# The second layer's down projection by seven block products instead of eight

## The chip, the cores and the metric

One core of a Trainium2 chip. The time is the device time of one execution in microseconds. TensorE (PE) multiplies matrices, VectorE (DVE), ScalarE (ACT) and GpSimd (POOL) work on rows of 128 partitions, and SyncE (SP) issues most of the transfers (DMAs). Each engine runs its own list of instructions in order and waits on semaphores for the others.

## The reference

Two layers of a backbone over 512 tokens of 1024 channels, batch 1. Each layer is a mixer (layer 0: long convolution and neighbourhood attention; layer 1: Conformer convolution) and then a feed-forward part, each between two RMS norms with shift, scale and gate. The change is in the feed-forward part of layer 1:

```python
def conv_ffn(t, w_up, w_dw, b_dw, w_down):
    z = dwconv(t @ w_up, w_dw, b_dw)          # (512, 1024) @ (1024, 5632), 3 taps over tokens
    g, u = jnp.split(z, 2, axis=-1)
    return (jax.nn.silu(g) * u) @ w_down      # (512, 2816) @ (2816, 1024)
...
        y = conv_ffn(hn, ffn_w_up[layer], ffn_w_dw[layer], ffn_b_dw[layer], ffn_w_down[layer])
        h = h + gate2 * rms_norm(y, g_ffn_post[layer])
    return h
```

All is float32.

## The kernel before

**Products.** A float32 operand is cast to the type `float32r` (`hi`), and what the cast leaves off is kept as a second `float32r` tile (`lo`). `mm3` makes one product of three matmuls, hi x hi, hi x lo and lo x hi, lines 284 to 286, accumulated in PSUM. A matmul has 128 rows of the contraction, 128 columns of one operand and 512 of the other.

**The stream of weights.** `Stream` holds all weight tiles of the kernel in the order of their use, each 128 x 1024 (512 KB). `load` (line 295) has SP read a tile into one of 3 buffers `raw`; `split` casts it on ScalarE (line 301, `hi`) and subtracts on VectorE (line 305, `lo`) into two of the 8 buffers `w`, so that four weight tiles are held. `get(n)` hands out the next tile and splits n tiles ahead, with three loads ahead of that. Tiles that have to stay (`wkeep`, named `wk`) go to other pools.

**The feed-forward part, `ffn(l, ...)`.** The up part makes 22 channel blocks i, each with a gate tile and a value tile: 24 matmuls into `pz`, then the 3-tap convolution (ScalarE line 983, VectorE 984 and 985), Silu (1383) and the product into `gu` (1387), where `gu[j]` holds blocks 2j and 2j+1 as 128 channels x 512 tokens. The down part is `gemm_td`: `act(k)` splits one block of `gu` into `gs` (lines 1420, 1421). For the first 16 blocks k, each weight tile serves all four chunks of 128 tokens and both halves of 512 outputs, 24 matmuls; for the last 6 (`KEEP`), the tiles are kept and the chunks are finished one after the other, in two halves of 18 matmuls each. `acc` are the eight PSUM tiles. When chunk t is done, `after(t, acc[t])` calls `post_chunk`: the square sum on ScalarE (line 426), the root on GpSimd (417, 421), the gain and the sum with `h` on VectorE (555, 560), and the output is sent (621).

**Order.** `bg` is a list of generators, of which `bg_step(n)` runs n steps: a weight tile of the up part is followed by two steps (`nbg` = 2). In layer 1 the list holds `mod_gate(1, 2)`, which reads 8 tiles of 512 KB by way of `raw`. A scheduler puts the instructions of each engine into an order from a timeline of its own; inside `tc.manual_schedule` an engine keeps the order of the code.

Of the kernel before, what the change touches and what calls it, by code (L numbers as in the profile page):

```python
# [239 lines left out]
def backbone_kernel(ctx: ExitStack, tc: tile.TileContext, a, cols, out, dump=None, stop=None, mark=lambda s: None):  # L240
# [51 lines left out]

    def load(src):
        r = rpool.tile([P, 1024], F32, name=nm("raw"), tag="raw")
        SP.dma_start(r, src)
        return r

    def split(r, alloc):
        mk = alloc or (lambda: w4(F32R, (P, 1024)))
# [1 line left out]
        A.copy(hi, r)  # L301
        with ExitStack() as queued:
            if behind:
                queued.enter_context(tc.issue_after(behind[0]))
            V.tensor_tensor(lo, r, f(hi), op=ALU.subtract)  # L305
# [165 lines left out]
    def mod_gate(l, which):  # L471
        p0 = 2 if which == 1 else 5
        binit = s4(F32, (P, 1024), "binit")
        G.memset(binit, 0.0)
# [898 lines left out]
        return  # L1373


    def ffn(l, hT, late, after, nxt, nbg):
# [37 lines left out]
        dmp(f"gu{l}", gu[0])  # L1414
        mark(f"down{l}")

        def act(k):
# [2 lines left out]
            A.copy(t_[:, 0], src)  # L1420
            V.tensor_tensor(t_[:, 1], src, f(t_[:, 0]), op=ALU.subtract)  # L1421
# [241 lines left out]
```

## Time and profile before

| | us |
|---|---|
| median of 3 runs | 1251.58 (1250.80 to 1252.73) |
| profiled execution | 1254.67 |
| its span, first to last instruction | 1252.9 |
| busy in the span: PE / DVE / ACT / POOL | 1238.9 / 815.9 / 509.2 / 81.2 |
| mean granted TensorE clock | 0.999 |
| first matmul of the layer 1 down part, from the span's start | 1126.37 |

Rows of the profile are in microseconds from the span's start. "L284 PE MATMUL acc<-w,gs" is an instruction of line 284 on TensorE that writes the tile `acc` from `w` and `gs`; "<-" in brackets names what ended the wait ahead of it. A busy time counts overlapping work of one engine once.

### The profile page before, as it was taken

How to read it: one execution, taken by the hardware profiler on the slowest of the kernel's cores; microseconds unless marked ns; L12 is line 12 of the kernel's file. 1: busy time of each engine (PE TensorE's matmuls, PEld its weight loads, DVE VectorE, ACT ScalarE, POOL GpSimd, SP SyncE). 2: the span in 40 equal slices, each digit the busy share in tenths (PEclk: the TensorE clock that was granted, in tenths of full speed). 3: DMA queues.
4: the chain of work that ended last, by engine and by line, in shares of the span. 5: the costliest groups of instructions: out<-in, count | busy, mean ns of one | idle time of the engine just before them, and what ended most of it. 6: DMA issues, size and time to landing. Idle time of an engine off the chain costs nothing.

```text
span 1252.9 us, 15592 instructions
## 1 busy us (share of the span) xinstructions
PE 1238.9 (99%) x6090; PEld 1028.7 (82%) x6090; DVE 815.9 (65%) x1085; ACT 509.2 (41%) x794; POOL 81.2 (6%) x151
## 2 busy tenths in 40 slices
PE   9999999999999999999999999999999999999997
PEld 6688888888898888787888888887988888888886
DVE  6577795876567788778534567787687555565223
ACT  6543234575353332436223442234534333344221
POOL 3300000241200000000000100001100000000001
PEclk9999999999999999999999999999999999999999
DMA  9546334734036577764334332120264333333221
GB/s 349 199 137 183 120 116 158 234 139 141 29 113 210 182 239 233 235 202 149 118 115 154 103 126 68 34 87 32 83 224 147 101 97 91 99 101 101 86 83 67
DMA packets 48089, 171.82 MB, mean 137 GB/s; under 512 B 5771, under 2 KB 5899, under 8 KB 48016
## 3 DMA queue, kind: packets, MB, share of 16 engines
q1 hardware_dynamic: 47652, 170.10, 42.1%
q8 instruction: 48, 0.79, 0.2%
q0 software_dynamic: 176, 0.40, 0.1%
q10 hardware_dynamic: 188, 0.33, 0.1%
q14 instruction: 25, 0.20, 0.0%
HBM read 167.92 MB, written 2.10 MB: 136 GB/s over the span
## 4 chain that ended last, share of the span: by engine, by line
PE 70%; DMA 12%; DVE 11%; ACT 3%; issue 3%; POOL 0%; SPq 0%; DVEq 0%; POOLq 0%; ACTq 0%
PE pz L284 10%; PE pz L285 10%; PE pz L286 10%; PE acc L286 8%; PE acc L285 8%; PE acc L284 8%; DMA raw<-in_wup 4%; DVE w L305 4%; DMA raw<-in_wcol 3%; DMA raw<-in_wgate 3%; PE pg L284 2%; PE pg L286 2%; PE pg L285 2%; ACT w L301 2%; DVE acc L448 2%
## 5 line engine op out<-in xcount | busy, mean ns | idle before, releaser
L286 PE MATMUL pz<-hTh,w 128*128 128x512 f32 (+1 forms) x920 | 345.3, 376 | 0.9 <-DVE w L305 0.9
L285 PE MATMUL pz<-hTl,w 128*128 128x512 f32 (+1 forms) x920 | 345.4, 376 | 0.0
L284 PE MATMUL pz<-hTh,w 128*128 128x512 f32 (+1 forms) x920 | 344.8, 377 | 0.6 <-DVE hTh L539 0.5
L305 DVE TENSOR_TENSOR w<-raw,w 128x1024 fp32r<-128x1024 f32 x159 | 193.9, 1222 | 200.3 <-ACT w L301 199.9
L301 ACT CAST w<-raw 128x1024 fp32r<-128x1024 f32 x159 | 166.5, 1051 | 337.8 <-PE pz L285 130.6
L286 PEld LDWEIGHTS pz<-hTh,w 128*128 128x128 f32 x920 | 173.8, 189 | 33.1 <-DVE w L305 1.8
L284 PEld LDWEIGHTS pz<-hTh,w 128*128 128x128 f32 x920 | 173.0, 189 | 31.3 <-DVE hTh L539 1.0
L285 PEld LDWEIGHTS pz<-hTl,w 128*128 128x128 f32 x920 | 173.8, 189 | 30.2 <-DVE hTl L540 0.4
L448 DVE SCALAR_TENSOR_TENSOR acc<-raw,sc,acc 128x1024 f32<-128x1024 f32 x74 | 95.0, 1284 | 44.5 <-DMA raw<-in_wcol 24.8
L285 PE MATMUL acc<-w,gs 128*128 128x512 f32 x256 | 99.6, 389 | 0.0
L286 PE MATMUL acc<-w,gs 128*128 128x512 f32 x256 | 98.4, 390 | 0.4 <-DVE gs L1421 0.4
L284 PE MATMUL acc<-w,gs 128*128 128x512 f32 x256 | 97.0, 389 | 0.0
L983 ACT ACTIVATE cv<-pz,pk 128x512 f32<-128x512 f32 x88 | 67.5, 773 | 0.0
L985 DVE SCALAR_TENSOR_TENSOR cv<-pz,pk,cv 128x511 f32<-128x511 f32 x88 | 65.5, 747 | 1.8
L984 DVE SCALAR_TENSOR_TENSOR cv<-pz,pk,cv 128x511 f32<-128x511 f32 x88 | 65.1, 744 | 0.2 <-ACT cv L983 0.2
L1383 ACT ACTIVATE cv<-cv 128x512 f32<-128x512 f32 x44 | 27.7, 629 | 81.3 <-DVE cv L985 81.2
L305 DVE TENSOR_TENSOR wk<-raw,wk 128x1024 fp32r<-128x1024 f32 x30 | 36.4, 1221 | 32.4 <-ACT wk L301 32.2
L286 PEld LDWEIGHTS acc<-w,gs 128*128 128x128 f32 x256 | 48.0, 188 | 10.7 <-DVE gs L1421 0.8
L284 PEld LDWEIGHTS acc<-w,gs 128*128 128x128 f32 x256 | 48.1, 188 | 10.2 <-DVE cv L985 0.2
L285 PEld LDWEIGHTS acc<-w,gs 128*128 128x128 f32 x256 | 48.0, 188 | 9.9
L555 DVE TENSOR_TENSOR py<-acc,gg 128x512 f32<-128x512 f32 x32 | 21.9, 687 | 46.9 <-ACT py L426 46.9
L301 ACT CAST wk<-raw 128x1024 fp32r<-128x1024 f32 x30 | 31.3, 1050 | 46.7 <-DMA raw<-in_wdn 27.3
(329 smaller groups left out, 1909.4 us busy)
## 6 DMA issues: line engine op xcount, KB each, us to landing
raw<-in_wup SPq DMA_DIRECT2D x88, 512.0 KB, 3.6
raw<-in_wcol SPq DMA_DIRECT2D x48, 512.0 KB, 4.2
raw<-in_wdn SPq DMA_DIRECT2D x44, 512.0 KB, 3.6
raw<-in_wgate SPq DMA_DIRECT2D x32, 512.0 KB, 4.3
raw<-in_pw SPq DMA_DIRECT2D x24, 512.0 KB, 4.3
raw<-in_win SPq DMA_DIRECT2D x20, 512.0 KB, 3.8
land<-in_wmod SPq DMA_DIRECT2D x16, 512.0 KB, 10.9
BM<-in_rpb SPq DMA_DIRECT2D x8, 512.0 KB, 4.2
```

The costliest lines, as they stand in the source:

```text
L284: PE.matmul(o, ah, bh, start=start, stop=False)
L285: PE.matmul(o, ah, bl, start=False, stop=False)
L286: PE.matmul(o, al, bh, start=False, stop=stop)
L301: A.copy(hi, r)
L305: V.tensor_tensor(lo, r, f(hi), op=ALU.subtract)
L448: V.scalar_tensor_tensor(acc, rs[k], ck_, init if k == 0 else acc, op0=ALU.mult, op1=ALU.add)
L555: V.tensor_tensor(p_[:, sl], y2[i], gg[:, sl], op=ALU.mult)
L983: A.activation(dst, pz, AF.Identity, bias=pc(bk, i), scale=pc(wk + "1", i))
L984: V.scalar_tensor_tensor(dst[:, 1:w], pz[:, 0:w - 1], pc(wk + "0", i), dst[:, 1:w], op0=ALU.mult, op1=ALU.add)
L985: V.scalar_tensor_tensor(dst[:, 0:w - 1], pz[:, 1:w], pc(wk + "2", i), dst[:, 0:w - 1], op0=ALU.mult, op1=ALU.add)
L1383: A.activation(cv[:, 0], cv[:, 0], AF.Silu, bias=0.0, scale=1.0)
```

## The change

Only the down part of layer 1 is changed. The 512 x 2816 activation A and the 2816 x 1024 weight B are cut into 2 x 2 blocks: tokens 0 to 255 and 256 to 511 (`H0`, `H1`), even and odd channel blocks (`gu[j][:, 0]`, `gu[j][:, 1]`), outputs 0 to 511 and 512 to 1023. Winograd's form of Strassen's scheme gives the four blocks of the result by seven products of 256 x 1408 by 1408 x 512 instead of eight, from sums of blocks. Three of the products take blocks of B as they are, four take sums (`PRODUCTS`).

- **Weights.** `wdb` holds the blocks in device memory, 128 x 5632 each. `sums_down()` makes the four sums in device memory, in six pieces of 1024 columns (the last 512): SP copies a block, and GpSimd issues a DMA that adds another block to it. It is a second generator in `bg`, 10 steps for a piece, 60 in all. A weight tile is now 128 x 1024 of one block, two k-blocks side by side, and each product has six, of which the last is half as wide: 42 tiles instead of 22.
- **Activations.** `blocks(j)` makes the sums on VectorE, one instruction of 512 columns and three of 256, when `gu[j]` is done in the up part. `parts(q, g)` splits what product q needs of a pair of k-blocks, `act_fast` keeps three pairs ahead.
- **Products.** `down_fast` runs the products in the order of `PRODUCTS`, with TensorE in the order of the code: for each tile two chunks x two k-blocks x three matmuls into two PSUM tiles `m`. VectorE sums the products (`sx`, `sw`, `y`; ScalarE copies the first into `s6`), and the seventh, which is finished chunk by chunk, gives the last half of chunks 2 and 3. Chunks 0 and 1 go through `after` during the seventh product.

```diff
-    a["wdn"] = g["ffn_w_down"].reshape(2, NFF, P, D)
+    wdn = g["ffn_w_down"].reshape(2, NFF, P, D)
+    a["wdn"] = wdn[:1]
+    a["wdb"] = wdn[1].reshape(11, 2, P, 2, 512).transpose(1, 3, 2, 0, 4).reshape(2, 2, P, 11 * 512)
...
+    wsum = {n: dram.tile([P, NP], F32, name=n) for n in ("b11_21", "b21_22", "b11_21_22", "b11_12_21_22")}
+    def sums_down():
+        b = a["wdb"]
+        for g in range(6):
+            cs = slice(g * 1024, min(g * 1024 + 1024, NP))
+            for copies, adds in (((("b11_21", b[0, 0]), ("b21_22", b[1, 0])),
+                                  ((("b11_21", b[1, 0]), ("b21_22", b[1, 1])),)),
+                                 ((("b11_21_22", b[0, 0]), ("b11_12_21_22", b[0, 1])),
+                                  ((("b11_21_22", wsum["b21_22"]),), (("b11_12_21_22", wsum["b11_21_22"]),)))):
+                with tc.issue_after(last_load[0]):
+                    for n, src in copies:
+                        SP.dma_start(wsum[n][:, cs], src[:, cs])
+                yield
+                yield
+                for add in adds:
+                    for n, src in add:
+                        G.dma_start(wsum[n][:, cs], src[:, cs], accum_op=ALU.add)
+                    yield
+                    yield
+    PRODUCTS = ("b11_21", "b11_12_21_22", "b11_21_22", (0, 0), (1, 1), "b21_22", (0, 1))
...
+            if fast and i % 2:
+                blocks(i // 2)
...
+        def blocks(j):
+            v = gu[j]
+            V.tensor_tensor(ee[j // 2][:, j % 2].rearrange("p (a b) -> p a b", a=2), v[:, :, H0], v[:, :, H1], op=ALU.add)
+            V.tensor_tensor(dd[j // 4][:, j % 4], v[:, 0, H0], v[:, 1, H0], op=ALU.subtract)
+            V.tensor_tensor(v[:, 0, H1], v[:, 0, H1], v[:, 1, H1], op=ALU.subtract)
+            V.tensor_tensor(v[:, 1, H0], v[:, 0, H0], v[:, 1, H1], op=ALU.add)
...
+            def prod(q, between={}):
+                m = [ps("m") for _ in range(2)]
+                held = []
+                for g in range(6):
+                    w_ = ws.get((2, 2, 2, 2, 2, 4, 4)[q])
+                    held.append((g, act_fast(q, g), w_))
+                    if g in between:
+                        between[g]()
+                    if q == 6 and 2 <= g < 5:
+                        continue
+                    for t in range(2):
+                        for g_, ac, (wh, wl) in held:
+                            for x, (ah, al) in enumerate(ac):
+                                ts_, ns = slice(t * P, (t + 1) * P), slice(x * 512, (x + 1) * 512)
+                                mm3(m[t], ah[:, ts_], al[:, ts_], wh[:, ns], wl[:, ns],
+                                    g_ == 0 and x == 0, g_ == 5)
+                        if q == 6 and g == 5:
+                            yield m[t]
+                    held = []
...
+            m6, = prod(0)
+            for t in range(2):
+                A.copy(s6[:, t], m6[t])
+            m2, = prod(1)
+            m1, = prod(2)
+                V.tensor_tensor(sx[:, t], m1[t], s6[:, t], op=ALU.subtract)
+                V.tensor_tensor(sw[:, t], sx[:, t], m2[t], op=ALU.subtract)
+            m7, = prod(3)
+                V.tensor_tensor(y[2 + t][:, 0], m7[t], s6[:, t], op=ALU.add)
+            m3, = prod(4)
+                V.tensor_tensor(sx[:, t], sx[:, t], m3[t], op=ALU.subtract)
+                V.tensor_tensor(y[t][:, 1], m2[t], sx[:, t], op=ALU.subtract)
+            m4, = prod(5)
+                V.tensor_tensor(y[t][:, 0], sx[:, t], m4[t], op=ALU.subtract)
+            for t, m5 in enumerate(prod(6, {1: first(0), 3: first(1)})):
+                V.tensor_tensor(y[2 + t][:, 1], m5, sw[:, t], op=ALU.add)
+                after(2 + t, [y[2 + t][:, 0], y[2 + t][:, 1]])
...
+        if fast:
+            bg_drain()
+            with tc.manual_schedule(engines={mybir.EngineType.PE}):
+                down_fast(after)
+            return
...
-    bg += [mod_gate(1, 2)]
+    bg += [mod_gate(1, 2), sums_down()]
     after, _, _ = stage_end(1, 2, last=True)
-    ffn(1, hT, late2, after, 0, 2)
+    ffn(1, hT, late2, after, 0, 2, fast=True)
```

The lines that follow are from the lists of instructions of the built programs, engine by engine, without times. A name's first number counts tiles. In the changed kernel lines stand further down: `mm3` is at 287 to 289, `load` at 298, `split` at 306 and 310, the split of activations at 1461 and 1463.

TensorE at the end of the up part and the first matmuls of the down part, before and after (`acc_1588`, `acc_1589` are the two output halves of chunk 0; `m_1594`, `m_1595` two chunks of product 0, each with two k-blocks of the first tile):

Before:

```order
L286 MATMUL pz_1581_9154<-hTh_1287_7129,w_1569_9077 128x512
L284 MATMUL acc_1588_9198<-w_1574_9113,gs_1585_9189 128x512
L285 MATMUL acc_1588_9198<-w_1575_9114,gs_1585_9189 128x512
L284 MATMUL acc_1589_9202<-w_1574_9113,gs_1585_9189 128x512
L285 MATMUL acc_1589_9202<-w_1575_9114,gs_1585_9189 128x512
L284 MATMUL acc_1590_9206<-w_1574_9113,gs_1585_9189 128x512
```

After:

```order
L289 MATMUL pz_1592_9271<-hTh_1287_7135,w_1580_9193 128x512
L287 MATMUL m_1594_9307<-w_1585_9230,gs_1571_9140 128x512
L288 MATMUL m_1594_9307<-w_1586_9231,gs_1571_9140 128x512
L289 MATMUL m_1594_9307<-w_1585_9230,gs_1571_9140 128x512
L287 MATMUL m_1594_9307<-w_1585_9230,gs_1571_9140 128x512
L288 MATMUL m_1594_9307<-w_1586_9231,gs_1571_9140 128x512
L289 MATMUL m_1594_9307<-w_1585_9230,gs_1571_9140 128x512
L287 MATMUL m_1595_9308<-w_1585_9230,gs_1571_9140 128x512
L288 MATMUL m_1595_9308<-w_1586_9231,gs_1571_9140 128x512
```

One weight tile (`w_1585`, `w_1586`) now meets 12 matmuls, and the next tile comes after them; before, the next one came after 24.

SP around the first loads of the down part, before and after (`raw` is the buffer, `in_wdn` the weight, `b11_21` and the like the sums in device memory; in brackets the semaphores that the row waits for, DMAHW of SP's own earlier DMAs, DMASW of GpSimd's):

Before:

```order
L295 DMA raw_1551_8937<-in_wup 128x1024 [waits DMAHW6_49,DVE_49]
L295 DMA raw_1557_8974<-in_wup 128x1024 [waits DMAHW7_49,DVE_49]
L295 DMA raw_1561_9009<-in_wdn 128x1024 [waits DMAHW0_49,DVE_49]
L295 DMA raw_1566_9045<-in_wdn 128x1024 [waits DMAHW1_49,DVE_49]
L295 DMA raw_1570_9080<-in_wdn 128x1024 [waits DMAHW2_49,DVE_49]
L295 DMA raw_1576_9117<-in_wdn 128x1024 [waits DMAHW3_49,DVE_49]
```

After:

```order
L298 DMA raw_1559_9027<-in_wup 128x1024 [waits DMAHW5_49,DMAHW0_49,DVE_49]
L358 DMA b11_21_78<-in_wdb 128x512 [waits DMAHW6_49]
L358 DMA b21_22_79<-in_wdb 128x512
L298 DMA raw_1565_9066<-in_wup 128x1024 [waits DMAHW3_49,DVE_49]
L298 DMA raw_1569_9103<-b11_21_78 128x1024 [waits DMAHW1_49,DMAHW4_49,DMASW4_49,DVE_49]
L358 DMA b11_21_22_80<-in_wdb 128x512 [waits DMAHW2_49]
L358 DMA b11_12_21_22_81<-in_wdb 128x512
L298 DMA raw_1577_9160<-b11_21_78 128x1024 [waits DMAHW5_49,DMASW0_49,DVE_49]
L298 DMA raw_1581_9196<-b11_21_78 128x1024 [waits DMAHW0_49,DMASW4_49,DVE_49]
L298 DMA raw_1587_9234<-b11_21_78 128x1024 [waits DMAHW1_49,DMAHW6_49,DMASW0_49,DVE_49]
L298 DMA raw_1591_9269<-b11_21_78 128x1024 [waits DMAHW4_49,DMAHW7_49,DMASW4_49,DVE_49]
```

The two pairs of copies for the last of the six pieces (128 x 512) stand between the loads, and a load of a sum waits for the add of its piece, which GpSimd issued.

ScalarE where product 0 ends, after; before, in the middle of the down part, no activation is split any more (`w` are weight tiles, `gs` activations, `s6` the copy of product 0):

Before:

```order
L301 CAST w_1600_9263<-raw_1580_9152 128x1024
L301 CAST w_1604_9296<-raw_1584_9187 128x1024
L301 CAST w_1608_9329<-raw_1598_9234 128x1024
L301 CAST w_1612_9362<-raw_1602_9267 128x1024
L301 CAST w_1616_9395<-raw_1606_9300 128x1024
```

After:

```order
L306 CAST w_1626_9462<-raw_1613_9398 128x1024
L1461 CAST gs_1641_9535<-gu_1371_7651 128x256
L1461 CAST gs_1641_9535<-gu_1392_7803 128x256
L1461 CAST gs_1645_9558<-gu_1417_7969 128x256
L1506 COPY s6_1619_9434<-m_1595_9308 128x512
L1461 CAST gs_1645_9558<-gu_1442_8132 128x256
L1461 CAST gs_1651_9577<-gu_1461_8285 128x256
L1461 CAST gs_1651_9577<-gu_1482_8441 128x256
L1461 CAST gs_1655_9600<-gu_1501_8595 128x256
L1461 CAST gs_1655_9600<-gu_1521_8749 128x256
L1461 CAST gs_1659_9623<-gu_1540_8902 128x256
L1461 CAST gs_1659_9623<-gu_1561_9057 128x256
```

Behind the tile `w_1626` of product 1 stand 12 casts of activations for later products and the second half of `s6`, and only then the next tile, `w_1630`, three rows further down.

More of the change, by code (lines that the diff above doesn't have):

```diff
@@ L293, in load @@
     def load(src):
-        r = rpool.tile([P, 1024], F32, name=nm("raw"), tag="raw")
-        SP.dma_start(r, src)
+        r = rpool.tile([P, 1024], F32, name=nm("raw"), tag="raw")[:, 0:math.prod(src.shape[1:])]
+        last_load[:] = [SP.dma_start(r, src).ins]
         return r
+    last_load = []
     def split(r, alloc):
         mk = alloc or (lambda: w4(F32R, (P, 1024)))
-        hi, lo = mk(), mk()
+        hi, lo = mk()[:, 0:r.shape[-1]], mk()[:, 0:r.shape[-1]]
         A.copy(hi, r)
@@ L335, in backbone_kernel @@
     ws.add([a["wout"][k] for k in range(8 - KEEP, 8)], wkeep)
+    dram = ctx.enter_context(tc.tile_pool(name="dram", bufs=1, space=bass.MemoryType.DRAM))
+    NP = 11 * 512
+    wsum = {n: dram.tile([P, NP], F32, name=n) for n in ("b11_21", "b21_22", "b11_21_22", "b11_12_21_22")}
[18 more added lines that the diff above has]
+    PRODUCTS = ("b11_21", "b11_12_21_22", "b11_21_22", (0, 0), (1, 1), "b21_22", (0, 1))
     def add_ffn(l):
         ws.add([flat(a["wup"][l, i, g], "p k n -> p (k n)") for i in range(NFF) for g in range(2)])
-        ws.add([a["wdn"][l, k] for k in range(NFF - KEEP)])
-        ws.add([a["wdn"][l, k] for k in range(NFF - KEEP, NFF)], wkeep)
+        if l == 0:
+            ws.add([a["wdn"][l, k] for k in range(NFF - KEEP)])
+            ws.add([a["wdn"][l, k] for k in range(NFF - KEEP, NFF)], wkeep)
+            return
+        for n in PRODUCTS:
+            src = wsum[n] if isinstance(n, str) else a["wdb"][n[0], n[1]]
+            src = [src[:, g * 1024:min(g * 1024 + 1024, NP)] for g in range(6)]
+            if n != PRODUCTS[-1]:
+                ws.add(src)
+            else:
+                ws.add(src, lambda: s4(F32R, (P, 1024), "wk"))
     add_ffn(0)
@@ L1373, in backbone_kernel, with ffn @@
         return
-    def ffn(l, hT, late, after, nxt, nbg):
+    def ffn(l, hT, late, after, nxt, nbg, fast=False):
         mark(f"ffn{l}")
@@ new lines, in parts @@
+        def parts(q, g):
+            n = min(2, 11 - 2 * g)
+            js = range(2 * g, 2 * g + n)
+            t_ = s4(F32R, n="gs")
+            hi, lo = (t_[:, x].rearrange("p (a b) -> p a b", a=2) for x in range(2))
+            if q < 4:
+                k, t = ((1, H1), (0, H0), (1, H0), (0, H1))[q]
+                srcs = [(slice(j % 2, j % 2 + 1), gu[j][:, k:k + 1, t]) for j in js]
+            elif q == 5:
+                srcs = [(slice(0, n), dd[g // 2][:, g % 2 * 2:g % 2 * 2 + n])]
+            else:
+                srcs = [(slice(0, n), ee[g][:, 0:n, H1 if q == 4 else H0])]
+            for sl, src in srcs:
+                A.copy(hi[:, sl], src)
+            for sl, src in srcs:
+                V.tensor_tensor(lo[:, sl], src, f(hi[:, sl]), op=ALU.subtract)
+            return [(hi[:, j % 2], lo[:, j % 2]) for j in js]
@@ new lines, in ffn, with act_fast, down_fast, pair @@
+        acts = {}
+        def act_fast(q, g, keep=False):
+            i0 = q * 6 + g
+            for i in range(i0, min(i0 + 3, 42)):
+                if i not in acts:
+                    acts[i] = parts(i // 6, i % 6)
+            return acts[i0] if keep else acts.pop(i0)
+        def down_fast(after):
+            def prod(q, between={}):
[17 more added lines that the diff above has]
+                    held = []
+                    bg_step(1)
+                if q < 6:
+                    yield m
+            def pair(n):
+                return s4(n=n)
+            m6, = prod(0)
+            s6 = pair("s6")
+            for t in range(2):
+                A.copy(s6[:, t], m6[t])
+            m2, = prod(1)
+            m1, = prod(2)
+            sx, sw = pair("sx"), pair("sw")
+            for t in range(2):
+                V.tensor_tensor(sx[:, t], m1[t], s6[:, t], op=ALU.subtract)
+            for t in range(2):
+                V.tensor_tensor(sw[:, t], sx[:, t], m2[t], op=ALU.subtract)
+            m7, = prod(3)
+            y = [s4(n="y") for _ in range(4)]
+            for t in range(2):
+                V.tensor_tensor(y[2 + t][:, 0], m7[t], s6[:, t], op=ALU.add)
+            m3, = prod(4)
+            for t in range(2):
+                V.tensor_tensor(sx[:, t], sx[:, t], m3[t], op=ALU.subtract)
+            for t in range(2):
+                V.tensor_tensor(y[t][:, 1], m2[t], sx[:, t], op=ALU.subtract)
+            m4, = prod(5)
+            act_fast(6, 0, keep=True)
+            for t in range(2):
+                V.tensor_tensor(y[t][:, 0], sx[:, t], m4[t], op=ALU.subtract)
+            def first(t):
+                return lambda: after(t, [y[t][:, 0], y[t][:, 1]])
+            for t, m5 in enumerate(prod(6, {1: first(0), 3: first(1)})):
+                V.tensor_tensor(y[2 + t][:, 1], m5, sw[:, t], op=ALU.add)
+                after(2 + t, [y[2 + t][:, 0], y[2 + t][:, 1]])
```

10 lines of the change are left out of this document (9 added, 1 removed).

## The prediction

> **What bounds the kernel now.** I read the page first: the share of each engine, and the chain that ended last.
>
> ```profile
> PE 1238.9 (99%) x6090; PEld 1028.7 (82%) x6090; DVE 815.9 (65%) x1085; ACT 509.2 (41%) x794; POOL 81.2 (6%) x151
> PE 70%; DMA 12%; DVE 11%; ACT 3%; issue 3%; POOL 0%; SPq 0%; DVEq 0%; POOLq 0%; ACTq 0%
> ```
>
> TensorE is busy for 99% of the span, so the bound is the number of matmuls in a row, wherever nothing else stops them. An average hides stages, so next I cut the last feed-forward layer into its up part and its down part.
>
> ```profile
> core 0: us, PE busy (x) PEld busy (x) DVE busy (x) ACT busy (x) POOL busy (x), PEclk, DMA share, GB/s
> 950.00:1120.00 170.00, 170.00 (x751) 140.76 (x750) 96.71 (x115) 63.68 (x78) 0.00 (x0) 1.00 0.33 98
> 1127.00:1246.00 119.00, 119.00 (x526) 98.36 (x525) 44.04 (x50) 32.37 (x49) 2.60 (x6) 1.00 0.25 84
> ```
>
> In both rows TensorE is busy for all of the time, at full granted clock, while VectorE is at 57% and 37%, ScalarE at 37% and 27%, GpSimd at nothing and the DMA engines at 33% and 25%. The down stage, which is what changes, is limited by TensorE alone; all else has room. Then the timeline, for where that stage starts and ends and what hangs behind it.
>
> ```profile
> 1126.14 0.39 PE L286 MATMUL pz<-hTh,w 128*128 128x512 f32 x1
> 1126.37 0.39 PE L284 MATMUL acc<-w,gs 128*128 128x512 f32 x1
> ...
> 1242.17 0.60 ACT L426 ACTIVATE py<-acc 128x512 f32<-128x512 f32 x1 [3.39 <-PE acc L286]
> 1246.25 0.60 ACT L426 ACTIVATE py<-acc 128x512 f32<-128x512 f32 x1 [3.39 <-PE acc L286]
> 1246.74 0.19 ACT L426 ACTIVATION_READ_ACCUMULATOR py<-acc 128x1 f32 x1
> 1247.03 0.30 POOL L417 TENSOR_SCALAR t<-t,t 128x1 f32<-128x1 f32 x1 [7.21 <-ACT py L426]
> 1247.42 0.56 POOL L421 TENSOR_TENSOR t<-t,nhalf 128x1 f32<-128x1 f32 x1
> 1246.97 0.69 DVE L555 TENSOR_TENSOR py<-acc,gg 128x512 f32<-128x512 f32 x1 [3.39 <-ACT py L426]
> 1248.01 1.41 DVE L560 SCALAR_TENSOR_TENSOR h<-py,t,h 128x512 f32<-128x512 f32 x2 [0.35 <-POOL t L421]
> 1249.46 0.39 ACTq L621 DMA_DIRECT2D out<-h  x1
> ```
>
> The down stage starts at 1126.37, with the first `acc` matmul. ScalarE's two rows at line 426 each start when a chunk's 18 matmuls are done: 4.08 us apart, so 0.2267 us a matmul. (The 0.39 of a row is pipelined latency.) The stage has 4 x 2 x 22 x 3 = 528 matmuls, 119.7 us, and 1126.37 + 119.7 = 1246.1 is where the last ACT row begins: no gap in it. Behind the last matmul hangs a tail of 1252.9 - 1246.25 = 6.65 us: square sum, its read, two GpSimd rows, two halves of `h`, the output's DMA. The profiled execution took 1254.67 us (span 1252.9); the median of the runs is 1251.58, 3.1 below, so a saving in the trace is taken off 1251.58.
>
> **The matmuls.** Seven products of 11 k-blocks x 2 token tiles x 3 make 462 matmuls of the same shape, 66 fewer: the lists of TensorE's instructions differ by 66 too. 66 x 0.2267 = **-14.96 us**, all on the path.
>
> **The tail.** The last half of the last chunk is now a sum, `y = m5 + sw` (line 1532), ahead of its square sum. The nearest row is the 0.69 of the 128x512 tensor_tensor from PSUM at 1246.97: **+0.7 us**. Chunk 2, whose last matmul is 21 matmuls (4.8 us) ahead of the end, needs 0.7 + 0.8 + 1.0 + 1.4 = 3.9 by those rows (its `h` in one piece taken as the two halves), so it is out of the way; its output goes 0.9 us before the last matmul's end, and the last two outputs start some 3 us after it.
>
> **Feeding the weights.** A weight tile served 24 matmuls (5.44 us); now it serves 12 (2.72), with 42 loads instead of 22. Two things could fail: the engines' work for each product, and the round trip of a buffer. First the engines, by the step from one row's start to the next one's.
>
> ```profile
> 1099.14 1.05 ACT L301 CAST w<-raw 128x1024 fp32r<-128x1024 f32 x1 [3.71 <-PE pz L285]
> 1100.10 0.78 ACT L983 ACTIVATE cv<-pz,pk 128x512 f32<-128x512 f32 x1
> 1122.53 3.74 ACT L1420 CAST gs<-gu 128x512 fp32r<-128x512 f32 x7
> 1100.23 1.22 DVE L305 TENSOR_TENSOR w<-raw,w 128x1024 fp32r<-128x1024 f32 x1 [2.04 <-ACT w L301]
> 1101.37 0.74 DVE L984 SCALAR_TENSOR_TENSOR cv<-pz,pk,cv 128x511 f32<-128x511 f32 x1
> 1123.79 1.28 DVE L1421 TENSOR_TENSOR gs<-gu,gs 128x512 fp32r<-128x512 f32 x2
> 1124.99 0.74 DVE L985 SCALAR_TENSOR_TENSOR cv<-pz,pk,cv 128x511 f32<-128x511 f32 x1
> L545 ACT ACTIVATE X<-pt,col,col 128x256 f32<-128x256 f32 x56 | 26.6, 574 | 25.8 <-PE pt L533 24.3 <-PE pt L960 1.5
> ```
>
> A cast of a weight tile takes ScalarE 0.96 (1099.14 to 1100.10), its rest VectorE 1.14 (1100.23 to 1101.37); activations of 512 columns 0.53 (3.74 / 7) and 0.60 (123.79 to 124.99, halved). For 256 columns no row of this kind exists. By the two lengths (each 512 columns add 0.43 and 0.54) it would be about 0.31 and 0.33, an estimate; the upper end is the 0.57 of the slowest 256-column ACT row, from PSUM, and the lower end is half of the 512 one. I take 0.31 and 0.33, for the source is SBUF as in the two rows they come from. A product (66 matmuls, 14.96 us) then costs ScalarE 5 x 0.96 + 0.53 + 11 x 0.31 = 8.7 and VectorE 5 x 1.14 + 0.60 + 11 x 0.33 = 9.9, plus up to six 0.6 sums of products: 13.5. Both fit. VectorE's new sums in the up stage, 11 x (0.60 + 3 x 0.33) = 17.5 us over 170, lift it from 57% to 67%, behind TensorE: cost 0.
>
> Now the round trip.
>
> ```profile
> 1096.04 101.79 SPq L295 DMA_DIRECT2D raw<-in_wdn  x22
> DMA to landing us min/median/max: 3.4/3.6/5.4
> 410.00:490.00 80.00, 80.00 (x355) 66.23 (x354) 65.41 (x71) 26.40 (x33) 0.95 (x1) 1.00 0.67 219
> ```
>
> Three `raw` buffers turn: landing 3.6, cast 1.05, rest 1.22, some 0.4 for three hand-overs (estimate) = 6.3, or 2.1 us a load; wanted is one in 7 x 14.96 / 42 = 2.49. So it holds, with 0.4 in hand. That the chip keeps up such a rate without TensorE stopping is in the last row: 219 GB/s with TensorE busy for all 80 us, against 0.524 MB / 2.49 = 210 GB/s here.
>
> Queues are in order, so a lump ahead of a weight tile counts more than a mean. The largest that I find stands on ScalarE behind product 0: `w_1626`, then 12 activation casts and a half of `s6`, then `w_1630`. Counted from product 0's end: `s6` 0.3, seven casts 2.5, `w_1626` 3.5, the lump 12 x 0.31 + 0.53 = 7.7, `w_1630` 8.8, its rest on VectorE 10.0. TensorE wants it after four groups, 10.9 + 0.2. It fits by 1.1; with 0.57 for 256 columns it comes 3.7 late. VectorE's waits for a finished product (`sx`, `y`) have weight tiles queued behind them, but those are three groups (8 us) ahead when a product starts, and I find the sums (0.6 each) pass in that time. For stalls of this kind I take **+0.8 us**, between 0 and 3.7 and nearer to 0 as the 256-column estimate is.
>
> **The weight sums.** 24 copies on SP's queue and 24 accumulating DMAs on GpSimd's. No row shows an accumulating DMA, nor one from device memory to itself; the nearest are these.
>
> ```profile
> 1.24 0.75 POOL L381 DMA_DIRECT2D zt<-in_qrow  x1 [0.81 <-POOLq L1659]
> 1222.56 0.30 POOL L417 TENSOR_SCALAR t<-t,t 128x1 f32<-128x1 f32 x1 [329.90 <-ACT py L426]
> land<-in_wmod SPq DMA_DIRECT2D x16, 512.0 KB, 10.9
> w4x<-in_fw POOLq DMA_DIRECT2D x2, 128.0 KB, 4.0
> ```
>
> GpSimd has nothing else to do until 1222.56 (idle 329.9 before), so 0.75 an issue costs nothing. SP's copies stand behind loads whose buffers were cast three tiles (16 us) before use, so even 10.9 to landing, the value in the full prologue queue, is covered in the up stage: cost 0. What must hold is the deadline. The copies begin 27 loads ahead of the first load of a sum: 1096.04 - 27 x 5.44 = 949. For each of six pieces GpSimd waits for two landings in turn (the third add reads the second's result, the fourth the third's). The sixth piece of the first sum is wanted at about 1123, after 11 landings; the last add at about 1142, after 12. So an add may take (1123 - 949) / 11 = 15.8 us. Bounds: 3.6 (a load of the size) to 10.9 (the same under load); the 128 KB DMA of that queue took 4.0. I take 6, nearer to the quiet rows, for the stage's DMA share is 33%. Cost 0.
>
> The DMA engines themselves: raw loads take share 0.33 at 98 GB/s; 11.5 MB copied over 174 us are 66 GB/s, at the same price 0.22, and the adds, which also read where they write, 0.22 to 0.45: 0.77 to 1.0 in all. Under 1 by my value, but close.
>
> The Trainium skill speaks against this term: "DMA: Bandwidth & Descriptors", section "Issuing engines are not separate DMA queues", says that transfers of all queues share the same 16 engines and interleave, and its "Latency and other measured facts" gives copies between HBM tensors 207 to 214 GB/s. By 214 the copies and adds alone would hold the engines for 2 x 11.5 / 0.214 = 108 us of the 174, an estimate, so 0.62 + 0.33 = 0.95; the sum stays -13.5 by it, with less room. No run here shows it yet.
>
> **Sum:** -14.96 + 0.7 + 0.8 = -13.5 (1241.2 for the profiled execution), so 1251.58 - 13.5 = **1238.1 us**.
>
> **Rivals.** *Feed.* If landing were the 5.4 of the slowest wdn load, as the sums' last DMAs or each other's crowd would make it, the turn is 8.1 / 3 = 2.69 against 2.49, and 42 loads lose 8.4 us: 1246.5. Against it: the median is 3.6 and the 219 GB/s row. With the ScalarE lump at its upper end instead (3.7 for 0.8) it is 1241.0.
> *Adds too late, slower.* Place: the first load of product 0's last piece, which waits on SP for GpSimd's add. Each us over 15.8 costs 11. At 17.2 the gain is gone. If an add, which moves its bytes three times, took twice the 10.9, 21.8 us, the kernel would wait 66 us: 1304. Against it: 10.9 was with nine tenths of the DMA engines busy by a queue of 16 loads, and here adds wait for each other, so at most two are in flight.
> *The change does nothing.* Excluded: 66 matmuls are gone from the order, and only a stall could hide that.
>
> **How the numbers follow.** Forecast (no stall over 4 us) 0.68; feed 0.15; adds late 0.12 (0.08 of it slower, 0.03 within 0.2%, 0.01 still faster); anything else 0.05 (0.01, 0.01, 0.03). A measurement here can tell 0.2%, 2.5 us. Faster: 0.68 + 0.14 + 0.01 + 0.01 = 0.84; same: 0.01 + 0.03 + 0.01 = 0.05; slower: 0.08 + 0.03 = 0.11. Range: low 1235.8 is the lowest run (1250.8) less 14.96 without tail or stall; high 1247.5 takes in the feed case and a us of spread. Outside stay the late adds and half of the rest, under 0.16.
>
> **What would show it.** In the trace after: the last stage's windows with TensorE busy throughout and 462 matmuls in about 105 us; 12 matmuls between weight tiles; no wait of TensorE on a `w` at line 310 over 1 us, above all not in product 1's fifth group; adds that land within 10 us, the last before product 1 ends; a tail of 7.3 us. I am wrong if SP idles on GpSimd's DMAs at the start of the stage, if landing of a `raw` there is 5 us or more, or if 256-column casts take over 0.5.

## The result, and the profile after

The changed kernel takes 1241.28 us (median of four runs, 1239.77 to 1242.31) against 1251.19 for the kernel before, measured beside it: 9.9 us less, a ratio of 0.992 with a 95% interval of 0.9902 to 0.9937. Forecast were 1238.1 us and 13.5 less, in a range from 1235.8 to 1247.5. It is faster, within the range, and 3.6 us of the gain are missing. The profiled execution has a span of 1238.0 and took 1239.77.

The page of the changed kernel, its line of engines:

```profile
PE 1222.3 (99%) x6024; PEld 1016.8 (82%) x6024; DVE 872.7 (70%) x1203; ACT 539.0 (44%) x856; POOL 104.7 (8%) x175
```

66 matmul rows are gone and TensorE is still at 99%. Next the windows: the up part, and of the down part the first, the sixth and the last product.

```profile
950.00:1120.00 170.00, 170.00 (x751) 140.73 (x751) 109.93 (x152) 66.00 (x87) 19.45 (x24) 1.00 0.83 226
1122.00:1137.00 15.00, 15.00 (x68) 12.43 (x67) 10.93 (x18) 8.60 (x14) 0.00 (x0) 1.00 0.51 145
1197.00:1212.00 15.00, 15.00 (x68) 12.43 (x67) 12.04 (x16) 8.42 (x13) 0.00 (x0) 1.00 0.67 200
1212.00:1227.50 15.50, 15.05 (x67) 12.01 (x65) 14.49 (x21) 9.46 (x22) 4.74 (x5) 1.00 0.30 112
```

TensorE never stops in the up part, though the DMA share there went from 0.33 to 0.83. In the last product VectorE works for 14.49 of 15.5 us, more than in any other, and TensorE loses half a microsecond. The timeline gives the first product matmul, the one that came late, and the last:

```profile
1122.12 0.39 PE L287 MATMUL m<-w,gs 128*128 128x512 f32 x1
...
1212.94 0.50 PE L289 MATMUL m<-wk,gs 128*128 128x512 f32 x1 [0.45 <-DVE gs L1463]
...
1227.36 0.39 PE L289 MATMUL m<-wk,gs 128*128 128x512 f32 x1
```

462 matmuls in steps of 0.2267 us take 104.5 us from the first start to the last; here it is 105.24, so TensorE stopped for 0.7, at the start of the last product, for a split of activations. From the last start to the end of the span it is 1238.0 - 1227.36 = 10.64, where the kernel before needs 7.06 (1252.9 less 1245.84, its last matmul's start by 527 steps of 0.2267 from 1126.37; the span is given to 0.1, so every tail in this document is good to 0.05). So from the first matmul of the down part to the end:

| us | before | changed | difference | forecast |
|---|---|---|---|---|
| matmuls | 119.47 | 104.51 | -14.96 | -14.96 |
| stops of TensorE | 0 | 0.73 | +0.7 | +0.8 |
| last matmul's start to the end | 7.06 | 10.64 | +3.6 | +0.7 |
| sum | 126.5 | 115.9 | -10.65 | -13.5 |

Against the forecast this table lacks 2.9 us, and all of it is in the last row, 3.6 for 0.7. The spans differ by 14.9, because the first matmul of the down part also came 4.25 us earlier than before. That is no gain of the change: in the eleven profiles below that contain it, all the same up to there but for the weight sums in one, it starts anywhere from 1119.81 to 1125.21, and at 1123.24 in the kernel before with sums (experiment 4). So I compare from that matmul on.

The missing piece hangs behind the last matmul. The timeline there:

```profile
1222.23 1.28 DVE L601 SCALAR_TENSOR_TENSOR h<-py,t,h 128x1024 f32<-128x1024 f32 x1
1223.43 0.69 DVE L596 TENSOR_TENSOR py<-y,gg 128x512 f32<-128x512 f32 x1
1224.03 1.28 DVE L601 SCALAR_TENSOR_TENSOR h<-py,t,h 128x1024 f32<-128x1024 f32 x1
1225.22 0.69 DVE L1532 TENSOR_TENSOR y<-m,sw 128x512 f32<-128x512 f32 x1
...
1228.30 1.29 DVE L601 SCALAR_TENSOR_TENSOR h<-py,t,h 128x1024 f32<-128x1024 f32 x1 [0.84 <-POOL t L462]
1229.50 0.69 DVE L596 TENSOR_TENSOR py<-y,gg 128x512 f32<-128x512 f32 x1
1230.10 0.69 DVE L1532 TENSOR_TENSOR y<-m,sw 128x512 f32<-128x512 f32 x1
1230.88 0.63 ACT L467 ACTIVATE py<-y 128x512 f32<-128x512 f32 x1 [3.54 <-DVE y L1532]
...
1231.64 0.69 DVE L596 TENSOR_TENSOR py<-y,gg 128x512 f32<-128x512 f32 x1 [0.85 <-ACT py L467]
1231.70 0.79 POOL L458 TENSOR_SCALAR t<-t,t 128x1 f32<-128x1 f32 x1 [3.44 <-ACT py L467]
1232.58 0.56 POOL L462 TENSOR_TENSOR t<-t,nhalf 128x1 f32<-128x1 f32 x1
1233.17 1.41 DVE L601 SCALAR_TENSOR_TENSOR h<-py,t,h 128x512 f32<-128x512 f32 x2 [0.84 <-POOL t L462]
1234.62 0.38 ACTq L662 DMA_DIRECT2D out<-h  x1
```

The two `y` rows at line 1532 are the sums of chunks 2 and 3. Chunk 2's last matmul starts 21 steps ahead of the last, at 1222.60, and by the 0.41 us that the square sum followed its matmul before, its `y` could start at 1223.01. It starts at 1225.22, 2.2 late, directly behind the `h` rows of chunks 0 and 1. From chunk 2's `y` to chunk 3's it is 4.88, for chunk 2's own gate and `h` with their two waits stand between them. Chunk 3's matmuls take nearly as long (4.76), so nothing is caught up, and chunk 3's `y` is 2.33 late too: 1230.10 against 1227.77. The rest of the tail is 0.78 from a `y` to its square sum, and 0.49 more in GpSimd's `tensor_scalar`: 0.79 here, 0.30 in the rows of before. 2.33 + 0.78 + 0.49 = 3.6, the whole difference of the last row.

The sums of weights, by the lines of their DMAs, first the adds (the last twelve by their own row, the landing of all 24):

```profile
L363 POOL DMA_DIRECT2D b<-b x12: 802/812/814, 963.8 to 1102.6; - x12
...
DMA to landing us min/median/max: 4.7/6.4/10.5
```

Then the copies:

```profile
L358 SPq DMA_DIRECT2D b<-in_wdb x24: 495/590/1067, 944.4 to 1092.7; - x24
...
DMA to landing us min/median/max: 4.7/7.9/9.5
```

And the loads of weights, from 940 to 1090 in the up part:

```profile
L298 SPq DMA_DIRECT2D raw<-in_wup x28: 328/333/337, 941.2 to 1086.4; - x28
...
DMA to landing us min/median/max: 4.0/5.4/8.8
```

An add lands after 6.4 us (forecast 6, allowed 15.8; the slowest took 10.5, where the prediction named 10 as the most). The last one was issued at 1102.6 and is there by 1113.1 even at the slowest landing, 9 us ahead of the first product matmul. The loads of the up part land in 5.4 instead of 3.6, and TensorE does not wait for it.

### The profile page after: what moved, and what is told of

It is laid out like the page before. It is cut to its first block, busy times and chain, and to the rows that moved or that the text cites. A ratio compares the mean times of both kernels' runs of the same rounds, so it can differ in the third digit from the quotient of the medians.

```text
span 1238.0 us, 15798 instructions
## 1 busy us (share of the span) xinstructions
PE 1222.3 (99%) x6024; PEld 1016.8 (82%) x6024; DVE 872.7 (70%) x1203; ACT 539.0 (44%) x856; POOL 104.7 (8%) x175
## 4 chain that ended last, share of the span: by engine, by line
PE 86%; DVE 7%; DMA 4%; issue 2%; ACT 1%; POOL 0%; SPq 0%; DVEq 0%; POOLq 0%; ACTq 0%
PE pz L287 15%; PE pz L288 15%; PE pz L289 15%; PE acc L289 5%; PE acc L287 5%; PE acc L288 5%; PE pg L287 2%; PE pg L288 2%; PE pg L289 2%; DMA raw<-in_wcol 2%; PE m L287 2%; PE m L288 2%; PE m L289 2%; PE po L1319 1%; DVE w L310 1%
## 5 line engine op out<-in xcount | busy, mean ns | idle before, releaser
L310 DVE TENSOR_TENSOR w<-raw,w 128x1024 fp32r<-128x1024 f32 x179 | 215.0, 1205 | 172.9 <-ACT w L306 170.7
L306 ACT CAST w<-raw 128x1024 fp32r<-128x1024 f32 x179 | 185.0, 1037 | 322.8 <-PE pz L288 139.6
L287 PE MATMUL m<-w,gs 128*128 128x512 f32 x132 | 51.3, 389 | 0.0
L288 PE MATMUL m<-w,gs 128*128 128x512 f32 x132 | 51.3, 389 | 0.0
L289 PE MATMUL m<-w,gs 128*128 128x512 f32 x132 | 51.3, 389 | 0.0
L310 DVE TENSOR_TENSOR wk<-raw,wk 128x1024 fp32r<-128x1024 f32 (+1 forms) x30 | 35.9, 1205 | 21.8 <-ACT wk L306 21.5
L288 PE MATMUL acc<-w,gs 128*128 128x512 f32 x128 | 49.8, 389 | 0.0
L289 PE MATMUL acc<-w,gs 128*128 128x512 f32 x128 | 49.1, 389 | 0.0
L287 PE MATMUL acc<-w,gs 128*128 128x512 f32 x128 | 48.5, 389 | 0.0
L306 ACT CAST wk<-raw 128x1024 fp32r<-128x1024 f32 (+1 forms) x30 | 30.9, 1037 | 37.4 <-DMA raw<-in_wdn 13.7
L458 POOL TENSOR_SCALAR t<-t,t 128x1 f32<-128x1 f32 x19 | 10.3, 541 | 398.0 <-ACT py L467 389.4
```

The costliest lines, as they stand in the source:

```text
L287: PE.matmul(o, ah, bh, start=start, stop=False)
L288: PE.matmul(o, ah, bl, start=False, stop=False)
L289: PE.matmul(o, al, bh, start=False, stop=stop)
L458: G.tensor_scalar(v, sums[0], sums[1], EPS, op0=ALU.add, op1=ALU.add)
```

## The experiments

In all of them three numbers are read from the profile: how late chunk 2's `y` starts (its start less 0.41, against its matmuls), the same for chunk 3's, and the tail, from the last `m` matmul's start to the end of the span. In the changed kernel's first profile they are 2.2, 2.3 and 10.64; in two later ones (experiments 8 and 12) 3.8, 3.9 and 12.2. Each experiment has one profile. The diffs are shortened to what the edit does.

### 1. The gate of chunks 0 and 1 left out

```diff
-            V.tensor_tensor(p_[:, sl], y2[i], gg[:, sl], op=ALU.mult)
+            if not (last and t < 2):
+                V.tensor_tensor(p_[:, sl], y2[i], gg[:, sl], op=ALU.mult)
```

> The four VectorE products with the gate (py = y * gg) of chunks 0 and 1 are left out in the last stage, so that their h is summed from the square in py; VectorE has 4 x 0.6 = 2.4 us less to do during the last product, all else stands. Measure: from the first m matmul to the end of the span, 115.9 us in the changed kernel. Theory (chunk 2's y stands on VectorE behind the work for chunks 0 and 1, and drags chunk 3's y with it): chunk 2's y starts when its matmuls are done, 2.2 us earlier, and the last y 2.2 us earlier: 113.7, median 2.2 below the changed kernel's, 1239.1. Rival (the late weight tiles of the last product set it, VectorE's work of chunks 0 and 1 fits into waits): 115.9 within 0.3. Rival (a sum at the end costs this much by itself): 115.9 too, with chunk 2's y earlier and chunk 3's not.

1241.49 us (ratio 0.9908, 0.9893 to 0.9924): no gain, so the expectation missed. Chunk 2's `y` is 1.4 late, the tail 9.82. That is 0.8 less than in the first profile, but 2.4 less than in experiments 8 and 12, as much as was left out. TensorE lost 2.3 in stops in this execution, and that hid it. VectorE's rows:

```profile
1222.85 1.28 DVE L602 SCALAR_TENSOR_TENSOR h<-py,t,h 128x1024 f32<-128x1024 f32 x1 [0.86 <-POOL t L462]
...
1225.24 1.28 DVE L602 SCALAR_TENSOR_TENSOR h<-py,t,h 128x1024 f32<-128x1024 f32 x1 [0.77 <-POOL t L462]
...
1227.04 0.69 DVE L1533 TENSOR_TENSOR y<-m,sw 128x512 f32<-128x512 f32 x1
```

Both `h` rows wait for GpSimd, and chunk 2's `y` behind them. So the 1.4 that are left are not VectorE's amount of work. How much of the lateness the left-out work made, 0.8 or 2.4, one profile does not tell.

### 2. Activations split five pairs ahead

```diff
-            for i in range(i0, min(i0 + 3, 42)):
+            for i in range(i0, min(i0 + (3, 5)[q > 4], 42)):
```

> In products 5 and 6 the activations are split five pairs of k-blocks ahead instead of three; the work is the same. Theory (VectorE is full in the last product, 14.5 of 15.5 us): two splits of activations (0.6 each) move from the last product into product 5, where VectorE waits for weight casts, and the stop of TensorE of 0.7 us at the start of the last product, which waited for such a split, goes: from the first m matmul to the end 115.9 - 0.7 - 1.2 = 114.0. Rival (weight tiles come too late, and VectorE waits for them in its queue whatever stands between): the stop stays and the total is 115.9 within 0.3.

1241.97 us (0.9914, 0.9897 to 0.993). There is no stop of TensorE, as forecast: 104.49 us from first to last matmul. The tail is 11.94, longer than in the first profile and 0.3 shorter than in experiments 8 and 12, with chunk 2's `y` 3.5 late: again both `h` rows wait for GpSimd (0.86 and 0.85). The theory was right on the stop and wrong on the tail.

### 3 and 4. The weight sums taken away, and made for nobody

```diff
-            src = wsum[n] if isinstance(n, str) else a["wdb"][n[0], n[1]]
+            src = a["wdb"][...]          # a plain block for each
-    bg += [mod_gate(1, 2), sums_down()]
+    bg += [mod_gate(1, 2)]
```

> No sums of weight blocks are made: the 48 DMAs of the sums are left out, and the four products that take sums take plain blocks in their place, loads and matmuls as before. Theory (the sums lie beside TensorE and end in time): median the same within 0.2% of 1241.3, loads of the up part land in 3.6 us instead of 5.4, and the tail stays at 10.6 us behind the last matmul's start. Rival (the sums take DMA time that the loads need, and part of the missing 3.6 us of the gain goes there): 1 to 4 us faster.

1241.64 us, ratio 0.9918 (0.99 to 0.9937): the same as with them (0.992).

```diff
-    bg += [mod_gate(1, 2)]               # the kernel before
+    bg += [mod_gate(1, 2), sums_down()]
```

> The kernel before, with the sums of weight blocks made beside it and read by nobody: the same 48 DMAs in the second up part. Theory (they cost nothing): 1251.2 within 0.2%, loads of the up part land in 5 us or more and TensorE stays busy for the whole of 950 to 1120. Rival (they cost what is missing): 1 to 4 us slower.

1251.98 against 1251.72, ratio 0.9998 (0.9988 to 1.0009). The up part of the kernel before with the sums beside it:

```profile
950.00:1120.00 170.00, 170.00 (x751) 140.78 (x750) 95.97 (x114) 65.69 (x82) 19.64 (x24) 1.00 0.85 235
```

The DMA engines are at 0.85 instead of 0.33, and TensorE is busy for all 170 us. From both sides: the sums cost nothing that can be measured here. In experiment 3 the loads of the up part landed in 3.5 us again, in experiment 4 in 4.8 (expected 5 or more). In experiment 3 the tail was 12.55 us (expected 10.6) with chunk 2's `y` 3.8 late, so the tail does not come from the sums' DMAs either.

### 5. The same rows, two of them behind chunk 2's `y`

```diff
             for t, m5 in enumerate(prod(6, {1: first(0), 3: first(1)})):
-                V.tensor_tensor(y[2 + t][:, 1], m5, sw[:, t], op=ALU.add)
+                done = V.tensor_tensor(y[2 + t][:, 1], m5, sw[:, t], op=ALU.add).ins
+                if t == 0:
+                    with tc.issue_after(done):
+                        ...                # h of chunks 0 and 1
```

> The same instructions as the changed kernel; on VectorE the two h rows of chunks 0 and 1 stand behind chunk 2's y instead of ahead of it, nothing else moves but their two output DMAs. Measure: from the last m matmul's start to the end of the span, 10.64 us in the changed kernel, 7.06 for acc before. Theory (chunk 2's y, and through it chunk 3's, waits on VectorE behind h rows that wait for GpSimd): y of chunk 2 starts within 0.3 us of its matmuls' end, the y of chunk 3 some 0.65 us late (2 x 0.69, 4 x 0.6 and 3 x 1.2 us of VectorE rows in between, 5.4 us, where 4.8 are free) instead of 2.35: tail 8.9, median 1.7 below the changed kernel's. Rival (late weight tiles): tail 10.6 within 0.3, since no load, cast or split moves. Rival (a sum costs this by itself): 10.6 too.

1239.78 us (0.9906, 0.9891 to 0.9921); beside it on the same chip the changed kernel took 1241.02 (experiment 8). The single runs of the two overlap (1237.42 to 1242.66, and 1238.76 to 1241.97), so the medians alone do not show the 1.2 us; what follows is read from the profile. VectorE and GpSimd:

```profile
1215.70 5.12 POOL L458 TENSOR_SCALAR t<-t,t 128x1 f32<-128x1 f32 x1 [114.71 <-ACT py L467]
...
1218.76 1.89 DVE L596 TENSOR_TENSOR py<-y,gg 128x512 f32<-128x512 f32 x3
1220.97 0.69 DVE L1540 TENSOR_TENSOR y<-m,sw 128x512 f32<-128x512 f32 x1 [0.32 <-PE m L289]
1221.58 1.28 DVE L603 SCALAR_TENSOR_TENSOR h<-py,t,h 128x1024 f32<-128x1024 f32 x1
1223.62 1.29 DVE L603 SCALAR_TENSOR_TENSOR h<-py,t,h 128x1024 f32<-128x1024 f32 x1 [0.77 <-POOL t L462]
```

Chunk 2's `y` now waits for TensorE and starts on time: the order on VectorE decided it, and the rivals, by which nothing would move, fall for that row. But the tail is 10.30, not 8.9: chunk 3's `y` is 2.05 late, because `h` of chunks 1 and 2 ahead of it wait 0.77 and 0.45 for GpSimd. (Without these waits it is 5.57 from one `y` to the other, near the 5.4 of the expectation, whose listed terms add up to 7.4.) And GpSimd's row on 128 x 1 numbers takes 5.12 us. It ends at 1220.82, 0.17 behind the end of VectorE's last row (1220.65) before its pause. That was the part of the theory still missing.

### 6 and 11. Three `h` rows moved, and five pairs ahead

As 5, with chunk 2's `h` behind chunk 3's `y`, and the line of experiment 2.

> As before this one, with chunk 2's h row behind chunk 3's y too, and the activations of the last two products split five pairs ahead. Theory: chunk 3's y starts when its matmuls are done, h of chunk 2 fits into VectorE's two waits behind it, tail 7.06 + 0.7 + 0.6 for the modelled ends = 8.3 us; no stop of TensorE at the start of the last product, so from the first m matmul to the end 104.5 + 8.3 = 112.8 against 115.9, and a median 3 us below the changed kernel's, about the 1238 that was forecast. Rival (late weight tiles): the stop of 0.7 stays and the tail is 10 or more.

> The sixth kernel once more, beside the changed kernel on the same chip. Theory: tail 8.5 within 0.3 us from the last m matmul's start, no stop of TensorE in the down part, median 3 to 4 us below the changed kernel's. Rival (its lead was a matter of the executions): tail or stop as in the changed kernel, medians within 1.5 us.

1237.25 us (0.9889, 0.9871 to 0.9906), and the second time 1237.51 (0.9892, 0.9876 to 0.9909). Beside them the changed kernel took 1241.02 and 1241.96: 3.8 and 4.4 less. VectorE the first time, and GpSimd's row of chunk 3:

```profile
1219.97 0.69 DVE L1540 TENSOR_TENSOR y<-m,sw 128x512 f32<-128x512 f32 x1 [0.61 <-PE m L289]
...
1224.73 0.69 DVE L1540 TENSOR_TENSOR y<-m,sw 128x512 f32<-128x512 f32 x1
1225.33 1.27 DVE L603 SCALAR_TENSOR_TENSOR h<-py,t,h 128x1024 f32<-128x1024 f32 x1
1226.33 0.97 POOL L458 TENSOR_SCALAR t<-t,t 128x1 f32<-128x1 f32 x1 [1.12 <-ACT py L467]
1226.53 0.68 DVE L596 TENSOR_TENSOR py<-y,gg 128x512 f32<-128x512 f32 x1
1227.97 1.41 DVE L603 SCALAR_TENSOR_TENSOR h<-py,t,h 128x512 f32<-128x512 f32 x2 [0.76 <-POOL t L462]
```

The last matmul starts at 1224.30, so chunk 3's `y` is on time to 0.02 us. The tail is 8.50 (forecast 8.3; 8.49 the second time), TensorE does not stop, and from the first matmul to the end it is 112.99 both times: 13.54 below the kernel before. This version beats both kernels. It changes no arithmetic.

### 7. The gate of chunks 0 and 1 on GpSimd

```diff
-            V.tensor_tensor(p_[:, sl], y2[i], gg[:, sl], op=ALU.mult)
+            (G if last and t < 2 else V).tensor_tensor(p_[:, sl], y2[i], gg[:, sl], op=ALU.mult)
```

> The four products with the gate of chunks 0 and 1 are made by GpSimd instead of VectorE, which has 2.4 us less to do in the last product; chunk 2's y stands behind the h of chunk 0 alone. What such a product costs on GpSimd no row shows. Theory (what stands ahead of chunk 2's y decides): the h of chunk 0 waits for GpSimd's t, which now stands behind two products there; with 1 us for each the tail is about 9, with 2.5 us about 12. Rival (VectorE's amount of work decides, not its order): 2.2 below 10.64, 8.4.

1242.38 us (0.9929, 0.9916 to 0.9943), tail 12.41, chunk 2's `y` 2.4 late and chunk 3's 4.2. Two such products took GpSimd 5.02 and 3.52 us, by which the theory forecast a tail of about 12:

```profile
1219.74 5.02 POOL L597 TENSOR_TENSOR py<-y,gg 128x512 f32<-128x512 f32 x2 [114.25 <-ACT py L467]
```

VectorE had 2.4 us less to do and waited 3.48 for GpSimd in one piece. The rival, that the amount of work alone decides, would have given 8.4, or 9.8 counted from the 12.2 of experiments 8 and 12; it falls.

### 8 and 12. The changed kernel again

> The changed kernel once more, on the same chip as the three runs beside it. Theory: tail 10.6 within 0.4, since the order on VectorE is fixed and its waits come from the same rows; the first m matmul may start some us earlier or later, as the stages ahead of the change do. Rival (the tail hangs on how late the weight tiles land in an execution): tail between 8 and 13, and a stop of another length at the last product's start.

> The changed kernel for the third time. Theory (chunk 2's y stands behind two h rows that wait for GpSimd, and GpSimd gets its turn only in VectorE's gaps): tail between 10 and 12.5 us, by how VectorE's rows fall; GpSimd's first 128x1 row ends within 0.3 us of a gap of VectorE. Rival (fixed by the order alone): 10.6 or 12.2 exactly.

1241.02 us (0.9911, 0.9896 to 0.9926) and 1241.96 (0.9922, 0.9906 to 0.9937). The tails are 12.20 and 12.21, with chunk 2's `y` 3.8 late in both; the stops 0.9 and 1.1. The expectation of 10.6 within 0.4 for the eighth run missed: the first profile, of the fastest of its four runs, had the short tail. Experiments 3, 9 and 10 have the same order ahead of chunk 2's `y`, and it is 3.8, 3.5 and 3.8 late there, so 2.2 is the exception. The 12.21 of the twelfth run fits its expectation and its rival alike and does not tell them apart. GpSimd's and VectorE's rows of the eighth run, with chunk 2's `y`:

```profile
1218.40 4.50 POOL L458 TENSOR_SCALAR t<-t,t 128x1 f32<-128x1 f32 x1 [115.79 <-ACT py L467]
...
1221.45 1.28 DVE L596 TENSOR_TENSOR py<-y,gg 128x512 f32<-128x512 f32 x2
1223.59 1.28 DVE L601 SCALAR_TENSOR_TENSOR h<-py,t,h 128x1024 f32<-128x1024 f32 x1 [0.86 <-POOL t L462]
...
1227.44 0.68 DVE L1532 TENSOR_TENSOR y<-m,sw 128x512 f32<-128x512 f32 x1
```

VectorE is busy without a pause up to 1222.73, GpSimd's row ends at 1222.90, then comes its power, then `h`. In the first profile GpSimd had its turn after 1.26 us, between two VectorE rows; here and in the twelfth (4.68 us) only at the pause. With 12.2 for the tail and 0.9 and 1.1 for stops the gain from the first matmul on is 9.0 and 8.8 us, with the first profile's values 10.65. The medians say 9.9, 10.2 and 8.4.

### 9. One row's source

```diff
-            V.tensor_tensor(p_[:, sl], y2[i], gg[:, sl], op=ALU.mult)     # chunk 3, second half
+            V.tensor_tensor(p_[:, sl], m5, gg[:, sl], op=ALU.mult)        # PSUM, without sw
```

> The changed kernel, in which the last VectorE product with the gate (second half of chunk 3) reads the seventh product m in PSUM in place of y in SBUF; the sum y is still made and squared, so only the source of this one row differs (sw is left out of that product). Measure: GpSimd's 128x1 tensor_scalar of chunk 3, which runs beside that row and took 0.79 us in all eight kernels after the change, 0.30 in the kernel before; and chunk 3's y start to the end of the span, 7.85 to 7.90 us. Theory (GpSimd is held while VectorE reads two tiles in SBUF): 0.30 us, and 7.4 to the end. Rival (GpSimd's row is longer for another reason, such as its start behind idle time): 0.79 and 7.9.

```profile
1233.59 0.69 DVE L596 TENSOR_TENSOR py<-m,gg 128x512 f32<-128x512 f32 x1 [0.85 <-ACT py L467]
1233.66 0.30 POOL L458 TENSOR_SCALAR t<-t,t 128x1 f32<-128x1 f32 x1 [3.44 <-ACT py L467]
```

0.30 instead of 0.79, in the one execution (1241.21 us), with a VectorE row of the same 0.69 beside it; from chunk 3's `y` to the end it is 7.34 (forecast 7.4) instead of 7.9. The expectation puts 0.79 and 7.85 to 7.90 down for all eight kernels so far; experiment 6 had 0.97 and 8.0, and experiment 3 had 8.2 to the end. Two rows that nobody arranged agree: in experiments 6 and 11 a GpSimd row beside chunk 2's `y`, which reads `m` in PSUM, took 0.30 too. So GpSimd is held by VectorE rows that read two tiles in SBUF, not by VectorE being busy. This is how the change reached GpSimd: in the kernel before, the gate row read the matmul's result in PSUM (`py<-acc,gg`), now it reads `y` in SBUF.

### 10. Chunk 3's root on VectorE

```diff
-        r = rstd(sums)                   # two 128x1 rows on GpSimd
+        r = rstd(sums, V if halves == 2 else G)   # a product in place of the power
```

> The changed kernel, in which the two 128x1 rows of chunk 3's reciprocal root stand on VectorE instead of GpSimd (the power is left out: a product with -0.5 in its place). Theory (two hand-overs, and GpSimd's 0.79 instead of 0.30, lie on the path behind the last y): h of chunk 3 starts about 2 us behind its y instead of 3.07, 6.8 us from y to the end. Rival (the hand-over from ScalarE's sum sets it): 3.0 and 7.9.

One execution, 1239.92 us. From chunk 3's `y` to its `h` it is 2.58 (forecast 2.0) instead of 3.07, and to the end 7.34 (forecast 6.8) instead of 7.9.

```profile
1232.29 0.69 DVE L596 TENSOR_TENSOR py<-y,gg 128x512 f32<-128x512 f32 x1 [0.85 <-ACT py L467]
1232.90 0.21 DVE L458 TENSOR_SCALAR t<-t,t 128x1 f32<-128x1 f32 x1
1233.14 0.16 DVE L462 TENSOR_TENSOR t<-t,nhalf 128x1 f32<-128x1 f32 x1
```

The two rows take 0.21 and 0.16, but stand behind the gate row, which waits until ScalarE has written its squares into the same tile. GpSimd's part of the tail is half a microsecond beside that wait. With the power it was not tried.

## Why the prediction was right, and where it was wrong

- **The matmuls** (-14.96): right, 462 in steps of 0.2267, 104.49 us from the first to the last start where TensorE did not stop (experiments 2, 6, 9 and 11).
- **Stalls** (+0.8): the size came out (0.7 to 1.1 in the three profiles of the changed kernel), but by luck, for the place was wrong. The lump of casts on ScalarE in product 1 stopped nothing: a 256-column activation takes ScalarE 0.32 (seven in 2.25) and VectorE 0.35 (seven in 2.43, first two rows below), near the 0.31 and 0.33 of the estimate. The stop came at the last product's start, for a split of activations that stood in VectorE's queue behind a weight tile whose load was late (last three rows). With five pairs ahead none of three profiles had a stop; with three pairs, eight of nine had stops, of 0.3 to 2.3 us, and experiment 9 had none.

```profile
1137.12 2.25 ACT L1461 CAST gs<-gu 128x256 fp32r<-128x256 f32 x7
...
1137.92 2.43 DVE L1463 TENSOR_TENSOR gs<-gu,gs 128x256 fp32r<-128x256 f32 x7
...
1209.98 1.05 ACT L306 CAST wk<-raw 128x1024 fp32r<-128x1024 f32 x1 [0.85 <-DMA raw<-in_wdb]
...
1211.06 1.23 DVE L310 TENSOR_TENSOR wk<-raw,wk 128x1024 fp32r<-128x1024 f32 x1 [0.64 <-ACT wk L306]
1212.20 0.69 DVE L1463 TENSOR_TENSOR gs<-ee,gs 128x512 fp32r<-128x512 f32 x1
```

- **The tail** (+0.7): the step that failed. "So it is out of the way", of chunk 2, let its `y` start when its matmuls end, and counted the rows behind it, not those ahead of it in VectorE's queue: the gates and `h` of chunks 0 and 1, which run in the same last product. They put it 2.2 to 3.8 late, and chunk 3's `y` as much. In experiments 8 and 12 (3.8) the `h` rows also wait for GpSimd's root, an engine that the prediction had read as doing nothing in this stage (2.60 of 119 us before). The term measured +3.6 in the first profile and +5.1 in the two others. With these rows moved behind (experiments 6 and 11) it is +1.4, and the sum -13.5, the forecast's number, though by other parts: no stall, and 0.7 more of tail. Of that 0.7 nearly all is GpSimd's longer row there (0.97 for 0.30).
- **The weight sums** (0): right, shown by leaving them out and by adding them to the kernel before. Copies landed in 7.9 (bound 10.9), adds in 6.4 (taken 6). The DMA share was 0.83, within 0.77 to 1.0. The Trainium skill, "DMA: Bandwidth & Descriptors", section "Issuing engines are not separate DMA queues", has all queues share the engines; the trace agrees, since the loads of SP landed in 5.4 instead of 3.6 while the copies and adds ran, and in 3.5 without them (experiment 3).
- **The rival Feed** had its condition half fulfilled, and little of its effect. 5.4 was reached in the up part, where a tile serves twice as many matmuls; in the down part (here from 1160 to 1195) the median was 4.0 at most, and no matmul waited for a weight tile itself; the late load ahead of the last product reached TensorE by way of the split. *Adds too late* did not come near; by its own 11 us for each us, the gain would be gone at 17.0, not 17.2.

```profile
DMA to landing us min/median/max: 3.6/4.0/6.5
```

## What to carry to other kernels

When a tail is priced, look at the queue of the engine that starts it: what stands ahead of its first row, and whom those rows wait for. A chunk that is finished early still costs, if its last rows are queued ahead of the row on the path; moving three rows and splitting two pairs earlier was worth about 4 us here. Taking 2.4 us of work away left the median where it was, though the tail in its one profile was 0.8 to 2.4 shorter. A change that turns a PSUM operand into an SBUF one may slow the engine beside it.
